# The attention and conv gates as Strassen products of tile pairs, a phase ahead of the attention, with the mixing gates alone filling the attention

## The chip, the cores and the metric

The kernel runs on one core of one Trainium2 chip. The metric is the device time of one execution in microseconds; lower is better. The times are medians of several runs. One execution was also recorded by the hardware profiler, and all views below are of that one.

## The reference, cut to what matters

One layer of a streaming encoder is applied to 1024 new frames and 32 frames of running streams, 1056 tokens in all (`TT`), with model width 1024. Ten groups of columns of one input projection are formed from the normed input `h`; the change concerns two of them, `ga` and `gb`:

```python
q, k, v, logf = ...                     # attention inputs; q and k are RMS-normed per head
ga = cols(OFF_GA, ATTN_WIDTH)           # gate of the attention branch
u  = cols(OFF_UA) * sigmoid(cols(OFF_UB))   # input of the causal depthwise convolution, 31 taps
gb = cols(OFF_GB, CONV_WIDTH)           # gate of the conv branch
ma, mb = cols(OFF_MA), cols(OFF_MB)     # gates that mix the two branches
...
ya = (o_attn * silu(ga)) @ w_pa
yb = (silu(layernorm(conv)) * silu(gb)) @ w_pb
y  = x + (sigmoid(ma) * ya + sigmoid(mb) * yb) @ w_out
```

All of it is float32. There are 16 heads of 64 channels, causal over the 1024 new frames.

## The kernel before, in words

Every float32 projection is made of three passes on TensorE: a matrix is held as a rounded part and a remainder (`xh`, `xl` for the input, `wh`, `wl` for a weight tile), and hi x hi, lo x hi and hi x lo are summed. `mms` (L102) issues these three matmuls for one of eight blocks of the contraction (`kt`). `steps` makes one tile of 128 output channels: three chunks of 352 tokens, each 8 blocks x 3 matmuls = 24 matmuls in one PSUM bank, and then an evacuation. One `yield` of `steps`, three matmuls, is called a step below, and 24 steps are a tile. A weight tile (512 KB) is loaded by `load_raw`, rounded by ScalarE (`wh`, L91), and its remainder is made by GpSimd (`wl`, L94) in `split_w`.

The stages follow one another in the program: `u` tiles and `v`, then `k` and `q` tiles (`qk`, with three further `u` tiles in between), the last `u` tile, the eight `ga` tiles, the attention, two tiles that are left over, and the three output projections. On TensorE the order is the program's order throughout. Up to the attention VectorE and ScalarE are in the program's order too; in the attention a scheduler orders them, and GpSimd and the DMA queue on SyncE are ordered by it everywhere.

The depthwise convolution runs on VectorE beside the projections: 30 `scalar_tensor_tensor` instructions a channel tile (the taps, L264). `beat()` is called at each step, adds a stage's rate (`R_U`, `R_QK`, `R_G`, `R_A`) to a credit and issues taps while the credit lasts. `later(n, fn)` runs `fn` n steps on.

The attention goes through `seq`: 16 heads x 8 blocks of 128 queries, and four `Sample`s for the running streams, 132 in all. A block has three parts: `scores` (matmuls into one of two `psS` buffers, the row maximum on VectorE L943, the exponential on ScalarE L946, the reciprocal L948, the scaling of `P` on GpSimd L949), `turn` (transposes of `P` on TensorE L966, copies of them by ScalarE L970 and VectorE L971), and `values` for two blocks at once (L982, L983; evacuated at L987, L988, gated at L993). In each round the program issues the scores of three blocks ahead, the turn of this block, four steps of gate projections from the generator `filler` (`fill(4)`), and the values of two blocks back. The filler holds 22 tiles (`NFILL`): the eight `gb` tiles and 14 of the 16 `ma` and `mb` tiles. It has one PSUM bank, `pq`; a chunk is evacuated by a copy (L771), and the next chunk writes the same bank:

```python
start(seq[0]); fill(8); start(seq[1]); fill(4); start(seq[2])
for n, b in enumerate(seq):
    start(seq[n + 3]); b.turn(); fill(4); seq[n - 2].values()      # cut
```

Eight steps are a chunk, so with fills of eight and four every chunk ends at the end of a fill. Head 0's operands are loaded while the `ga` tiles run.

## Time and profile before

| | |
|---|---|
| median of 3 runs | 1394.41 us (1393.71 to 1394.59) |
| span of the profiled execution, first to last instruction | 1392.1 us; its time as a run lies about 2.3 us above, by the median |
| TensorE busy | 1384.3 us, 99% of the span |
| VectorE, ScalarE, GpSimd busy | 906.5, 642.7, 623.2 us |
| granted TensorE clock | 1.000 |
| `ga` stage | about 510 to 598.6 us |
| attention | 598.6 to 1086.8 us |

A row of the timeline or of a group names the line, the engine, the operation, output and inputs by the program's names, shape and count. Matmuls are pipelined: a row's duration runs into the next row's, so the pace of a stream of matmuls is read from the distance of the starts, not from the durations.

### The profile page before, as it was taken

To read this page: it belongs to the slowest core of one execution; us is meant where nothing else is said; L and a number is where in the kernel's file an instruction comes from. 1 tells how busy PE (TensorE), PEld (TensorE's weight loads), DVE (VectorE), ACT (ScalarE), POOL (GpSimd) and SP (SyncE) were. 2 spreads that over 40 slices of the span, in tenths; PEclk is the share of its full clock that TensorE was granted. 3 is DMA by queue.
4 is the path that set the end of the run, shared out by engine and by line. 5 is a ranking of instruction groups with operands and counts; after the bars stand their busy time and mean duration, and the time that the engine had idled before them with its cause. 6 is when DMAs were issued, how large, how long until landed. Compare 5 with 4: busy or idle time off the path is not lost.

```text
span 1392.1 us, 24733 instructions
## 1 busy us (share of the span) xinstructions
PE 1384.3 (99%) x9382; PEld 1346.1 (97%) x9382; DVE 906.5 (65%) x1280; ACT 642.7 (46%) x1318; POOL 623.2 (45%) x669
## 2 busy tenths in 40 slices
PE   8999999999999999999999999999999999999999
PEld 7999999999999999999999999999999999999998
DVE  6687787888898999657766767655555487132111
ACT  6333434646464642245555556655555556222100
POOL 2324254657575875443333444343433257254320
PEclk9999999999999999999999999999999999999999
DMA  5253442424342374344545556454642779444431
GB/s 182 93 179 116 153 136 97 155 85 144 98 164 88 124 207 141 116 124 123 144 137 169 155 147 175 118 152 124 174 134 86 266 265 289 135 150 141 143 107 47
DMA packets 110615, 201.24 MB, mean 145 GB/s; under 512 B 17377, under 2 KB 74593, under 8 KB 110497
## 3 DMA queue, kind: packets, MB, share of 16 engines
q1 hardware_dynamic: 110352, 199.60, 45.7%
q8 instruction: 74, 1.21, 0.4%
q14 instruction: 45, 0.36, 0.1%
q10 hardware_dynamic: 144, 0.07, 0.0%
HBM read 129.78 MB, written 69.84 MB: 143 GB/s over the span
## 4 chain that ended last, share of the span: by engine, by line
PE 97%; DVE 1%; ACT 1%; DMA 0%; issue 0%; POOL 0%; SPq 0%; DVEq 0%; POOLq 0%; ACTq 0%
PE pj L102 71%; PE pjv L592 7%; PE ptr L966 5%; PE po L982 3%; PE po L983 3%; PE psS L938 3%; PE psS L939 2%; PE psS L941 1%; PE pst L716 1%; PE pst L715 1%; PE ptx L434 0%; DMA xtok<-xt 0%; ACT xh L436 0%; PE pjs L549 0%; DVE xl L437 0%
## 5 line engine op out<-in xcount | busy, mean ns | idle before, releaser
L102 PE MATMUL pj<-xh,wh 128*128 128x352 f32 (+2 forms) x1536 | 509.3, 332 | 0.4 <-ACT t L771 0.3
L102 PE MATMUL pj<-xl,wh 128*128 128x352 f32 (+2 forms) x1536 | 494.9, 322 | 0.2 <-DVE xl L437 0.2
L102 PE MATMUL pj<-xh,wl 128*128 128x352 f32 (+2 forms) x1536 | 493.2, 321 | 0.0
L94 POOL TENSOR_TENSOR wl<-raw,wh 128x384 fp32r<-128x384 f32 (+1 forms) x258 | 318.6, 1262 | 234.9 <-ACT wh L91 209.6
L264 DVE SCALAR_TENSOR_TENSOR y<-u,vec_t,y 128x1086 f32<-128x1086 f32 x240 | 378.3, 1577 | 11.5 <-ACT y L261 8.2
L102 PEld LDWEIGHTS pj<-xh,wh 128*128 128x128 f32 x1536 | 289.0, 188 | 3.4 <-issue 0.8
L102 PEld LDWEIGHTS pj<-xl,wh 128*128 128x128 f32 x1536 | 288.7, 188 | 1.4 <-DVE xl L437 1.2
L102 PEld LDWEIGHTS pj<-xh,wl 128*128 128x128 f32 x1536 | 289.4, 188 | 0.2 <-DVE wl L456 0.2
L949 POOL TENSOR_SCALAR P<-P,nm 128x128 f32<-128x128 f32 (+7 forms) x128 | 99.0, 773 | 230.6 <-DVE nm L948 203.1
L943 DVE TENSOR_REDUCE nm<-psS 128x1 f32<-128x128 f32 (+7 forms) x128 | 96.4, 754 | 71.9 <-PE psS L941 70.5
L91 ACT CAST wh<-raw 128x1024 fp32r<-128x1024 f32 x86 | 90.1, 1048 | 112.2 <-PE pj L102 81.0
L970 ACT CAST pth<-ptr 128x512 fp32r<-128x512 f32 (+1 forms) x192 | 89.1, 481 | 81.2 <-PE ptr L966 80.9
L971 DVE TENSOR_TENSOR ptl<-ptr,pth 128x512 fp32r<-128x512 f32 (+1 forms) x192 | 103.3, 550 | 24.0 <-ACT pth L970 22.3
L946 ACT ACTIVATE P<-psS,nm 128x128 f32<-128x128 f32 (+7 forms) x128 | 95.3, 744 | 35.0 <-DVE nm L943 30.3
L733 POOL TENSOR_TENSOR ql<-qn,qh 128x352 fp32r<-128x352 f32 (+1 forms) x48 | 64.6, 1346 | 69.2 <-ACT qh L732 49.8
L966 PE MATMUL ptr<-ident,P 128*128 128x128 f32 x576 | 85.0, 275 | 0.0
L982 PE MATMUL po<-pth,V 128*128 128x256 f32 x320 | 79.0, 283 | 0.0
L983 PE MATMUL po<-ptl,V 128*128 128x256 f32 x320 | 78.6, 281 | 0.0
L592 PE MATMUL pjv<-vwh,xh 128*128 128x260 f32 x256 | 72.5, 283 | 0.0
L592 PE MATMUL pjv<-vwl,xh 128*128 128x260 f32 x256 | 72.5, 283 | 0.0
L592 PE MATMUL pjv<-vwh,xl 128*128 128x260 f32 x256 | 72.3, 283 | 0.0
L938 PE MATMUL psS<-KB,QB 128*128 128x256 f32 (+2 forms) x192 | 67.9, 355 | 0.0
(213 smaller groups left out, 2460.8 us busy)
## 6 DMA issues: line engine op xcount, KB each, us to landing
raw<-wf SPq DMA_DIRECT2D x88, 512.0 KB
s_v<-vb SPq DMA_DIRECT2D x32, 256.0 KB
QB<-s_q SPq DMA_DIRECT2D x32, 256.0 KB
KB<-s_k SPq DMA_DIRECT2D x32, 256.0 KB
V<-s_v SPq DMA_DIRECT2D x16, 512.0 KB
kT<-qn SPq DMA_DIRECT2D x8, 528.0 KB
s_ga<-t SPq DMA_DIRECT2D x24, 176.0 KB
s_gb<-t SPq DMA_DIRECT2D x24, 176.0 KB
```

The lines of the kernel that those rows point to most:

```text
L94: nc.gpsimd.tensor_sub(wl[:, k0:k1, :], raw[:, k0:k1, :], f32(wh[:, k0:k1, :]))
L102: nc.tensor.matmul(ps, a[:, kt, :], b(kt, sl), start=(first and n == 0), stop=(last and n == N - 1))
L264: t = nc.vector.scalar_tensor_tensor(y, u[:, i:i + CW], w, y, op0=ALU.mult, op1=ALU.add)
L592: nc.tensor.matmul(ps[:, :VC], a, b, start=(n == 0), stop=(n == 23))
L938: nc.tensor.matmul(ps[:, b, :wm], QB[:, qsl], KB[:, ksl], start=True, stop=False)
L943: nc.vector.tensor_reduce(nm[:, 0:1], ps[:, :nb, :w], axis=AX.XY, op=ALU.max, negate=True)
L946: nc.scalar.activation(P[:, :nk].rearrange("p (b w) -> p b w", b=nb), ps[:, :nb, :w], AF.Exp, bias=nm[:, 0:1], accum_out=nm[:, 1:2])
L949: nc.gpsimd.tensor_scalar(P[:, :nk], P[:, :nk], nm[:, 2:3], 1.0, op0=ALU.mult, op1=ALU.mult)
L966: nc.tensor.transpose(pt[:, 128 * j:128 * j + 128], P[:, 128 * (4 * u + j):128 * (4 * u + j) + 128], ident)
L971: nc.vector.tensor_sub(ptl[:, js, qo], p3, f32(pth[:, js, qo]))
L982: nc.tensor.matmul(po[:, :256], V[:, j, :], pth[:, j, :], start=(j == 0), stop=False)
L983: nc.tensor.matmul(po[:, :256], V[:, j, :], ptl[:, j, :], start=False, stop=(j == njb - 1))
```

## The change

The 16 tiles of `ga` and `gb` are made as eight pairs of neighbouring tiles. A pair is a product of a 256 x 1024 weight matrix with the 1024 x 1056 input; cut in halves in each direction it is a 2 x 2 block product, and it is made with seven block products instead of eight (Winograd's form of Strassen's method). A block product is 4 contraction blocks x 3 passes x 2 chunks of 264 tokens, 24 matmuls; a pair is 168 matmuls of 264 columns where two tiles were 144 of 352.

The sums of quarters of the input (`xf`, and the third form, which is written over a quarter of `xh` and `xl`) are made once: `forms_of_x` in the `qk` stage on GpSimd and VectorE, `third_form` at the start of the first pair. The overwritten quarter is saved to `s_b` in DRAM and loaded back behind the last pair's fourth product. The sums of quarters of the weights (`sa`, `sb`) are made by VectorE for each pair, the rounding and remainders of seven half tiles by ScalarE and GpSimd, and the block products are combined at the evacuation, mostly by VectorE adds. All eight PSUM banks belong to the pairs in this phase.

All pairs run ahead of the attention. The filler of the attention then holds 14 tiles of `ma` and `mb`; the steps of a round are 4 or 5 (4.9 on average in the first 34 rounds, 4.5 afterwards) until the 14 tiles are used up. Head 0 is loaded behind the last pair, and the first eight filler steps stand ahead of the first scores. Several buffers move to a shared pool.

The diff, cut to its core:

```diff
-NFILL = 22
-R_U, R_V, R_QK, R_G, R_A = 0.25, 0.17, 0.19, 0.27, 0.12
+NFILL = 14
+R_U, R_V, R_QK, R_S, R_A = 0.25, 0.17, 0.19, 0.22, 0.12
+HT = TT // 2
+HC = HT // 2
+SPAIRS = [(g, 2 * i) for g in ("ga", "gb") for i in range(4)]
...
+    def forms_of_x():
+        xf.extend(ar.tile([128, 2, 4, HT], F32R, name="xf", tag=f"s{i}") for i in range(3))
+        for i, x in enumerate((xh, xl)):
+            nc.sync.dma_start(s_b[i], f32(x[:, 0:4, HT:]))
+        def part(j):
+            b11, b12, b21, b22 = [x32(nc.gpsimd, j + k, hf) for k in (0, 4) for hf in (0, 1)]
+            made = ((b11, 1), (b22, 2), (b21, 0))
+            def sums():
+                pace["credit"] -= 2.7
+                nc.vector.tensor_sub(b11, b12, b11)
+                nc.vector.tensor_sub(b22, b22, b11)
+                nc.vector.tensor_sub(b21, b21, b22)
+                for t, i in made:
+                    nc.scalar.copy(xf[i][:, 0, j, :], t)
+                later(5, lows)
...
+            later(26, sums)
...
+        if f == 5:
+            forms_of_x()
...
+    class Pair:
+        def split(self, i, src, n=2):
...
+            nc.scalar.copy(wh[:, :4 * n, :], src)
+            with tc.high_priority(offset=3000):
+                for k in range(0, 4 * n, 4):
+                    nc.gpsimd.tensor_sub(wl[:, k:k + 4, :], src[:, k:k + 4, :], f32(wh[:, k:k + 4, :]))
...
+        def product(self, i):
+            tag, wi, half, mov = PRODUCTS[i]
...
+            for c in range(2):
+                for kt in range(4):
+                    h, l = mov(kt, c)
+                    k = 4 * half + kt
+                    for n, (a, x) in enumerate(((wh, h), (wl, h), (wh, l))):
+                        nc.tensor.matmul(ps[:, c, :HC], a[:, k, :], x, ...)
+                    beat()
+                    yield
+            later(2, lambda: self.evac(i, ps[:, :, :HC]))
...
+    pps.close()
+    ps4 = pool("ps4", 1, stack=pS, space=PS)
+    pace["rate"] = R_S
+    for k, p in enumerate(pairs):
+        nxt = pairs[k + 1] if k + 1 < len(pairs) else None
+        later(2, lambda: p.made(5))
+        if k == 0:
+            pace["credit"] -= 5.0
+            later(1, lambda: third_form((0, 1)))
...
+        for i in range(7):
+            if nxt:
+                if i == 0:
+                    nxt.load()
+                for m, (ai, at) in enumerate(((3, 2), (4, 1), (5, 2), (5, 4), (6, 2))):
+                    if ai == i:
+                        later(at, lambda m=m: nxt.made(m))
+            for _ in p.product(i):
+                pass
+            if not nxt and i == 3:
+                for a, x in enumerate((xh, xl)):
+                    nc.sync.dma_start(f32(x[:, 0:4, HT:]), s_b[a])
...
-        if f == 5:
-            heads[0].load()
-        for _ in gate_steps("ga", f, pj):
-            pass
...
+    heads[0].load()
+    pq = pool("pq", 1, stack=p2, space=PS)
...
-    fills = [("gb", f) for f in range(8)] + [(g, f) for g in ("ma", "mb") for f in range(8)]
+    fills = [(g, f) for g in ("ma", "mb") for f in range(8)]
...
+    fill(8)
     start(seq[0])
-    fill(8)
+    fill(4)
     start(seq[1])
     fill(4)
     start(seq[2])
+    share = 0.0
     for n, b in enumerate(seq):
...
+        share += 4.9 if n < 34 else 4.5
+        n_fill = int(share)
+        share -= n_fill
...
             b.turn()
-            fill(4 if b.i > 2 or b.head.h != 8 else 0)
+            fill(n_fill)
```

More of the change, by code (lines that the diff above doesn't have):

```diff
@@ L488, in build @@
         plan.extend([("k", f), ("q", f)])
-    plan.extend([("ub", 7), ("ua", 7)] + [("ga", f) for f in range(8)] + [("gb", 0)])
+    plan.extend([("ub", 7), ("ua", 7)])
     V, G = nc.vector, nc.gpsimd
@@ L802, in build, with third_form, third_low @@
+    def third_form(js):
+        for j in js:
+            t, b = third[j]
+            nc.vector.tensor_sub(t, b, t)
+            nc.scalar.copy(xh[:, j, HT:], t)
+    def third_low(js):
+        for j in js:
+            nc.vector.tensor_sub(xl[:, j, HT:], third[j][0], f32(xh[:, j, HT:]))
     cvt[0] = u7p
     pace["rate"] = R_U
-    u_proj(7, pj)
-    assert not late
-    pqk.close()
-    pv.close()
-    hp = pool("hp", 2, stack=p2, side="right")
-    heads = [Head(h) for h in range(H)]
+    pS = ExitStack()
@@ L821, in build @@
     order.close()
+    pS.close()
     prw.close()
     pcv.close()
-    pps.close()
+    rawp[:] = [wp]
+    hp = pool("hp", 1, stack=p2, side="right")
+    heads = [Head(h) for h in range(H)]
+    heads[0].load()
+    pq = pool("pq", 1, stack=p2, space=PS)
     es.enter_context(tc.manual_schedule(engines={E.PE}))
```

186 lines of the change are left out of this document (153 added, 33 removed).

## The prediction

> **What bounds the kernel now.** I read the page first, then the busy times by stretch, then the chain that ended last.
>
> ```profile
> span 1392.1 us, 24733 instructions
> PE 1384.3 (99%) x9382; PEld 1346.1 (97%) x9382; DVE 906.5 (65%) x1280; ACT 642.7 (46%) x1318; POOL 623.2 (45%) x669
> PEclk9999999999999999999999999999999999999999
> PE 97%; DVE 1%; ACT 1%; DMA 0%; issue 0%; POOL 0%; SPq 0%; DVEq 0%; POOLq 0%; ACTq 0%
> ```
> ```profile
> core 0: us, PE busy (x) PEld busy (x) DVE busy (x) ACT busy (x) POOL busy (x), PEclk, DMA share, GB/s
> 510.00:600.00 90.00, 90.00 (x569) 89.96 (x568) 66.26 (x46) 23.91 (x37) 40.88 (x32) 1.00 0.48 141
> 900.00:1000.00 100.00, 100.00 (x745) 94.31 (x744) 53.98 (x121) 55.34 (x131) 36.21 (x67) 1.00 0.51 146
> ```
>
> TensorE is the chain, at the full granted clock, in the `ga` stage (510 to 600 us) and in the attention alike. So whatever shortens TensorE's stream shortens the kernel, and whatever makes TensorE wait lengthens it by as much. The attention has this cover only because filler steps stand in every round: in the second stretch VectorE and ScalarE are busy for 54 and 55 of 100 us. The change works on both sides: it takes columns from TensorE, and it takes eight tiles of filler out of the attention.
>
> **The products.** The pace comes from evacuations of a dense stream, each behind 24 matmuls: the `ga` chunks (352 columns) and those of `v` (260 columns).
>
> ```profile
> L769 ACT ACTIVATE t<-pj x12: 463/465/468, 534.0 to 575.9; 128x352 f32<-128x352 f32 x12
> L598 ACT COPY vf<-pjv x12: 372/372/375, 87.3 to 119.1; 128x256 f32<-128x256 f32 x12
> ```
>
> Eleven distances in 41.9 us are 3.81 us each, 158.7 ns a matmul; eleven in 31.8 us are 2.89 us, 120.5 ns a matmul. A column thus costs 0.415 ns, and a matmul of 264 columns 122.1 ns. Before, 16 tiles x 72 x 158.7 ns = 182.8 us; after, 8 pairs x 168 x 122.1 ns = 164.1 us: **18.7 us less**. So 7/8 of the columns is worth 10% of the time, since 192 more matmuls each pay a fixed part. If a column cost all there is (0.451 ns) it would be 22.7 us; these are the ends.
>
> **The switch of chunks inside a fill.** The filler has one PSUM bank. Before, chunks of eight steps end at the end of a fill, and scores, transposes or values stand ahead of the next chunk. The start of the attention shows a switch with little between:
>
> ```profile
> 602.61 0.33 PE L102 MATMUL pj<-xl,wh 128*128 128x352 f32 x1
> ...
> 603.01 0.45 ACT L771 COPY t<-pj 128x352 f32<-128x352 f32 x1 [1.01 <-ACT P L946]
> ...
> 603.52 0.43 PE L102 MATMUL pj<-xh,wh 128*128 128x352 f32 x1 [0.28 <-ACT t L771]
> ...
> 603.78 0.32 PE L102 MATMUL pj<-xh,wl 128*128 128x352 f32 x1
> ```
>
> From the start of a chunk's last matmul to that of the next chunk's first pass 0.91 us, with ScalarE idle beforehand; 0.16 us is the normal distance, so the switch costs 0.75 us, and 0.10 us more at the second matmul (0.26 instead of 0.16). The new fills are four or five steps, so chunk ends fall within them. In the built order of TensorE's instructions 32 of the 42 chunks of the attention begin right behind the previous chunk's last matmul. Nothing behind a waiting matmul can pass it on TensorE: the next scores, transposes and values are queued there, and VectorE, ScalarE and GpSimd wait for them. ScalarE is busy 55% of the time with operations of some 0.5 us, so I add 0.10 us for a copy that finds it busy: 32 x 0.95 = **30 us more**. Ends: 32 x 0.75 = 24 us, and 32 x 1.25 = 40 us where the copy mostly stands behind an exponential.
>
> **The half without filler.** 14 tiles are 336 steps. 16 go ahead of the first round, 34 rounds take 4.9, and the remaining 153 steps last 34 rounds at 4.5: the filler ends in round 69 of 132, which the built order shows too. The last 63 rounds have nothing but their own matmuls. What these heads cost now is read between the last evacuation of head 7 and that of head 15:
>
> ```profile
> L987 ACT COPY ot<-po x33: 363/365/371, 850.8 to 1087.0; 64x256 f32<-64x256 f32 x33
> ```
> ```profile
> L971 DVE TENSOR_TENSOR ptl<-ptr,pth 128x512 fp32r<-128x512 f32 (+2 forms) x94 | 51.0, 555 | 12.7 <-ACT pth L970 11.6 <-issue 0.4
> L949 POOL TENSOR_SCALAR P<-P,nm 128x640 f32<-128x640 f32 (+7 forms) x60 | 45.9, 765 | 116.7 <-DVE nm L948 97.3 <-PE ptr L966 7.6 <-PE pj L102 6.9
> L943 DVE TENSOR_REDUCE nm<-psS 128x1 f32<-128x768 f32 (+7 forms) x59 | 45.5, 772 | 30.7 <-PE psS L941 29.9 <-POOL ptl L957 0.3 <-POOL pth L956 0.3
> L946 ACT ACTIVATE P<-psS,nm 128x768 f32<-128x768 f32 (+7 forms) x59 | 44.7, 758 | 14.8 <-DVE nm L943 14.1
> L771 ACT COPY t<-pj 128x352 f32<-128x352 f32 x32 | 14.4, 450 | 13.3 <-PE pj L102 12.5
> L988 DVE TENSOR_TENSOR ot<-ot,po 64x256 f32<-64x256 f32 x32 | 13.3, 417 | 33.9 <-ACT ot L987 33.6
> L948 DVE RECIPROCAL nm<-nm 128x1 f32<-128x1 f32 x59 | 9.4, 160 | 17.5 <-ACT P L946 17.4
> L993 DVE TENSOR_TENSOR ot<-ot,ga 128x256 f32<-128x256 f32 x16 | 7.4, 461 | 0.4
> ```
>
> 236.2 us hold 32 chunks of 3.81 us, 122 us; TensorE's own work is 114 us. VectorE's five groups are 126.6 us. Without filler VectorE is therefore the longer engine, and even if it never paused the half would cost 127 - 114 = 13 us more. The other end comes from a gap that head 8's first blocks have in the filler now:
>
> ```profile
> 844.40 0.32 PE L102 MATMUL pj<-xl,wh 128*128 128x352 f32 x1
> ...
> 847.10 0.28 PE L966 MATMUL ptr<-ident,P 128*128 128x128 f32 x1
> ...
> 853.81 0.60 PE L966 MATMUL ptr<-ident,P 128*128 128x128 f32 x4
> ```
> ```profile
> 854.17 0.41 PE L102 MATMUL pj<-xh,wh 128*128 128x352 f32 x1
> ```
>
> From 844.56 (the end of the last step) to 854.17 are four rounds, 2.40 us a round, and they kept TensorE supplied, though it had some matmuls of the layer norm between. 62 rounds at that pace are 149 us, 35 us more than 114. Between 13 and 35 I take 143 us, **29 us more**, nearer the upper row, since VectorE in order, two score buffers and three transposed-block buffers leave some gaps. If rounds take longer than in that gap, it is a rival below. Here a rule of the Trainium skill speaks against the change: TensorE: Matmul & The Clock Gate, section "A second HAM failure mode: psum-queue depth-cycling", says that frequent short idles of TensorE between groups make its clock fall and recover. The granted clock is 1.00 in every row here, and no row has such idles for long, so that the trace does not decide it; the rival that it gives is priced below.
>
> **The seams and the loads beside the products.** Durations under load:
>
> ```profile
> L264 DVE SCALAR_TENSOR_TENSOR y<-u,vec_t,y x37: 1344/1351/3487, 509.7 to 574.8; 128x1086 f32<-128x1086 f32 x37
> L94 POOL TENSOR_TENSOR wl<-raw,wh x24: 734/1754/2068, 508.4 to 590.8; 128x384 fp32r<-128x384 f32 x16, 128x256 fp32r<-128x256 f32 x8
> L1123 DVE TENSOR_TENSOR y<-y,mean 128x1056 f32<-128x1056 f32 x8 | 14.3, 1785 | 0.0
> L971 DVE TENSOR_TENSOR ptl<-ptr,pth 128x512 fp32r<-128x512 f32 x96 | 65.6, 687 | 22.6 <-ACT pth L970 21.3 <-issue 0.4
> ```
>
> A pair lasts 20.5 us on TensorE. In it VectorE has seven or eight taps (8 x 1.35 = 10.8 us), four weight sums (like half of L1123, 4 x 0.87 = 3.5) and five adds from PSUM (like L971, 5 x 0.69 = 3.4): 17.7 us, 86%. GpSimd has seven remainders of 512 columns; at 1.75 us for 384 they are 2.34 us each, 16.4 us. Both fit, barely; half the slowest tap there (1.74 us) would make VectorE 20.8 us. I take 3 us for the phase, ends 0 and 16. The last pairs have few taps, and the weights are asked for some 8 us ahead. At the first pair GpSimd has seven remainders and two sums of the input in the 18 us from the middle of the last `u` tile to the fourth product: 16.4 + 2 x 2.4 = 21 us, so I take 3 us, ends 0 and 8. The sums of the input in the `qk` stage (16 on GpSimd, 24 operations on VectorE) are paced by the credit and take the place of taps; 1 us, ends 0 and 8. At the end of the attention the last values have no filler ahead of them: one transposed copy late, 2 us, ends 0 and 3.
>
> At the hand-over head 0's loads now stand on SyncE behind the last pair's last output, and in the built order the second half of them (the last keys) stands behind the output of the first filler chunk. A head's load now:
>
> ```profile
> 1008.76 0.45 SPq L786 DMA_DIRECT2D QB<-s_q  x1
> ...
> 1013.32 0.49 SPq L793 DMA_DIRECT2D KA<-s_ak  x1
> ```
>
> Issuing alone takes 5.0 us. The last pair's output is ready about 1 us behind its last matmul, and the first scores wait for all loads; TensorE has one chunk, 3.8 us, to run. 1 + 5 + some 3 us for the wait behind the chunk's output and the landing, less 3.8, is **5 us**, ends 2 and 10. The scores after them, the first transposes and head 1 are queued behind.
>
> **The sum.** -18.7 + 30 + 29 + 3 + 3 + 1 + 2 + 5 = +54 us. The span becomes 1392.1 + 54 = 1446 us; the runs' median lies 2.3 us above the span now, so 1394.4 + 54 = 1448 us.
>
> **The rivals.**
> 1. *The saving stands and the attention hides the rest: faster.* The switches and the half without filler would have to cost less than 18.7 - 14 = 5 us together; against it stand 0.75 us a switch and VectorE's 127 us against TensorE's 114. If ScalarE's copies and the scores ahead covered all of it, with 5 us at the seams, 1394.4 - 18.7 + 5 = 1381 us. It decides where a switch costs under 0.1 us and a round under 1.85 us. Chance 0.09, of which 0.02 is for seams of the full 14 us and a few switches, which end at no change.
> 2. *The floors alone.* Switches 24, the half 13, seams 5: +23 us, 1418 us. VectorE's pauses of 12.7 and 30.7 us in the rows above are waits for a TensorE that is itself full of filler, which speaks for it. Chance 0.20.
> 3. *The half without filler is bound by latency.* A block goes through maximum 0.77, exponential 0.76, reciprocal 0.16, scaling 0.77, then transposes and copies; with only three blocks ahead and two score buffers, waits behind other operations could make a round 2.9 us: 62 x 2.9 = 180 us, 66 instead of 29. That is +91 us, 1485 us; it decides from 2.4 us a round. Chance 0.18.
> 4. *The granted clock falls in that half*, since TensorE pauses at every block. At half the clock, TensorE's 114 us become 228; against 143 us that is 85 us more, 1533 us. The 1.00 in all rows speaks against it. Chance 0.03. The page of the Trainium skill named above gives such a fall.
> 5. *The change does not do what it says.* The built order has 1344 matmuls of 264 columns in one run, and no `gb` step in the attention, so only the promised time can be missing. No chance of its own.
>
> **How the numbers follow.** My forecast has 0.50. The range reaches from below rival 2 (1414 us) to above rival 3 (1490 us) and leaves out 1 and 4 and a part of the edges: 1414 to 1490. About 0.2% is what a measurement here can tell from no change, 2.8 us. Faster 0.07, within 0.2% 0.02 (both rival 1), slower 0.91 (all else).
>
> **What would show it.** Products at 2.9 us each between about 510 and 675 us; at the 32 switches distances of 0.9 to 1.1 us between filler matmuls, released by the copy; in the last third of the attention TensorE's own matmuls with waits for VectorE and ScalarE, VectorE busy near 90%, 2.2 to 2.4 us a round; a wait for head 0's load behind the first eight steps. I am wrong if the rounds without filler run at 1.9 us or the switches cost under 0.3 us.

## The result, and the profile after

The changed kernel takes **1501.85 us** (median of 4 runs, 1499.87 to 1504.09) where the kernel before takes 1394.5 us: ratio **1.077**, 95% interval 1.076 to 1.079. It is 107.4 us slower. The prediction said slower, by 54 us; the time lies 12 us above its range.

The page of the changed kernel, in the lines that answer to those shown of before:

```profile
span 1500.5 us, 25418 instructions
PE 1404.7 (94%) x9574; PEld 1339.9 (89%) x9574; DVE 1017.5 (68%) x1386; ACT 656.0 (44%) x1330; POOL 699.8 (47%) x699
PEclk9999999999999989999899999999999999999999
PE 45%; DVE 8%; issue 2%; ACT 2%; DMA 2%; POOL 0%; DVEq 0%; ACTq 0%; SPq 0%
```

TensorE is idle for 96 of 1500 us where it was idle for 8: it waits. The chain that ended last tells less here: its shares add up to 59%, since it leads back no further than 610 us; of what it covers TensorE is about three quarters, and VectorE comes next. The same two stretches as before, by windows (busy time of each engine with its instructions, granted clock, DMA share, GB/s):

```profile
core 0: us, PE busy (x) PEld busy (x) DVE busy (x) ACT busy (x) POOL busy (x), PEclk, DMA share, GB/s
510.00:600.00 90.00, 82.02 (x612) 81.21 (x611) 86.15 (x75) 32.48 (x47) 61.68 (x34) 0.94 0.24 86
900.00:1000.00 100.00, 92.28 (x621) 84.36 (x619) 56.76 (x110) 47.99 (x114) 33.81 (x61) 0.98 0.46 129
```

The first stretch now holds the first pairs, with VectorE busy 86 of 90 us; the second is in the filled half of the attention, and TensorE idles there too. What it waits for there is one row of the waits between 740 and 1038 us (total, times, longest):

```profile
PE pj L109 <- ACT t L816: 22.4, 31, 2.7
```

These are the ends of chunks inside a fill (32 with one at the start of the attention). The half without filler, first by the evacuations of the values in the same 64 rounds as before, then by its window and its longest waits:

```profile
L1200 ACT COPY ot<-po x33: 363/366/371, 1037.7 to 1195.3; 64x256 f32<-64x256 f32 x33
```
```profile
1038.00:1196.00 158.00, 130.41 (x976) 107.18 (x975) 122.78 (x287) 103.88 (x262) 55.36 (x121) 0.95 0.50 132
```
```profile
PE ptr L1179 <- DVE ptl L1184: 12.2, 15, 1.6
PE po L1195 <- DVE ptl L1184: 4.4, 6, 1.8
PE po L1195 <- DVE nm L1161: 3.9, 3, 1.9
PE po L1195 <- DVE ot L1206: 3.5, 2, 1.8
```

The 64 rounds take 157.6 us, 2.46 us each, where TensorE's own work is 114 us: 44 us lost. All waits in this window add up to 27 us. For the rest TensorE is busy longer than 114 us: the granted clock of 0.95 is some 16 us at half speed, at most 8 us of work by this estimate; what remains is not broken down. VectorE is named in the waits, yet it is busy only 122.8 of 158 us.

The places ahead of the attention, the first row from the kernel before, the rest from the changed kernel:

```profile
400.00:500.00 100.00, 100.00 (x628) 99.97 (x627) 90.08 (x83) 57.94 (x108) 72.05 (x48) 1.00 0.37 123
```
```profile
400.00:500.00 100.00, 91.55 (x550) 87.56 (x549) 93.69 (x83) 54.01 (x103) 84.82 (x59) 1.00 0.31 107
524.00:550.00 26.00, 18.48 (x119) 17.88 (x118) 25.60 (x25) 6.57 (x9) 16.75 (x10) 0.80 0.13 42
550.00:600.00 50.00, 49.54 (x407) 49.33 (x406) 47.78 (x41) 18.43 (x25) 33.37 (x16) 1.00 0.31 109
600.00:650.00 50.00, 47.87 (x392) 47.45 (x391) 49.03 (x41) 14.57 (x20) 37.93 (x20) 1.00 0.30 106
650.00:707.00 57.00, 54.29 (x441) 53.45 (x440) 43.10 (x39) 13.57 (x16) 29.98 (x19) 1.00 0.37 128
```

The counts of matmuls tell the loss: 78 fewer in the key stage, some 12 us at 0.16 us each; at the first pair 119 x 0.121 us = 14.4 of 26 us, 11.6 lost; in the other pairs, counted in the same way, 0.8, 2.7 and 3.7 us (7 in all). VectorE is busy 94 to 98% of each of these windows but the last, where it is 76%. The start of the kernel loses some 5 us as well: the first matmul of `v` stands at 77.0 us instead of 71.6. At the hand-over to the attention:

```profile
PE psS L1151 <- DMA KB<-s_k: 9.1, 1, 9.1
PE psS L1152 <- DMA KA<-s_k: 3.8, 1, 3.8
```
```profile
714.00:729.00 15.00, 5.18 (x19) 4.76 (x19) 1.70 (x3) 0.46 (x2) 1.38 (x1) 0.54 1.00 247
```

Head 0's keys are late by 9.1 and 3.8 us, and the granted clock is 0.54 in this stretch, so that the work between and behind the waits runs slowly as well; I put the loss at some 15 us.

### The profile page after: what moved, and what is told of

Same layout as the page of the kernel before. It is cut to its first block, busy times and chain, and to the rows that moved or that the text cites. A ratio compares the mean times of both kernels' runs of the same rounds, so it can differ in the third digit from the quotient of the medians.

```text
span 1500.5 us, 25418 instructions
## 1 busy us (share of the span) xinstructions
PE 1404.7 (94%) x9574; PEld 1339.9 (89%) x9574; DVE 1017.5 (68%) x1386; ACT 656.0 (44%) x1330; POOL 699.8 (47%) x699
## 4 chain that ended last, share of the span: by engine, by line
PE 45%; DVE 8%; issue 2%; ACT 2%; DMA 2%; POOL 0%; DVEq 0%; ACTq 0%; SPq 0%
PE pj L109 30%; PE po L1195 3%; PE ptr L1179 3%; PE po L1196 2%; DVE y L272 2%; PE psS L1151 2%; PE psS L1152 2%; DVE nm L1156 2%; PE ps L903 2%; DVE ptl L1184 1%; ACT t L816 1%; DMA QB<-s_q 1%; ACT P L1159 1%; PE psS L1154 1%; DMA KA<-s_k 0%
## 5 line engine op out<-in xcount | busy, mean ns | idle before, releaser
L109 PE MATMUL pj<-xh,wh 128*128 128x352 f32 (+3 forms) x1152 | 385.2, 334 | 27.1 <-ACT t L816 23.0
L272 DVE SCALAR_TENSOR_TENSOR y<-u,vec_t,y 128x1086 f32<-128x1086 f32 x240 | 393.7, 1640 | 13.8 <-ACT y L269 11.4
L109 PE MATMUL pj<-xh,wl 128*128 128x352 f32 (+3 forms) x1152 | 372.0, 323 | 1.8 <-POOL wl L101 1.8
L109 PE MATMUL pj<-xl,wh 128*128 128x352 f32 (+3 forms) x1152 | 373.1, 324 | 0.3 <-DVE xl L445 0.2
L101 POOL TENSOR_TENSOR wl<-raw,wh 128x384 fp32r<-128x384 f32 (+1 forms) x210 | 257.1, 1251 | 201.7 <-ACT wh L98 184.6
L109 PEld LDWEIGHTS pj<-xh,wh 128*128 128x128 f32 x1152 | 217.5, 189 | 39.0 <-ACT t L816 32.2
L109 PEld LDWEIGHTS pj<-xh,wl 128*128 128x128 f32 x1152 | 218.1, 189 | 3.7 <-POOL wl L101 3.5
L109 PEld LDWEIGHTS pj<-xl,wh 128*128 128x128 f32 x1152 | 217.6, 189 | 1.8 <-DVE xl L445 1.8
L903 PE MATMUL ps<-xf,wh 128*128 128x264 f32 x384 | 75.0, 290 | 8.5 <-DVE u L318 5.9
L1179 PEld LDWEIGHTS ptr<-ident,P 128*128 128x128 f32 x576 | 64.0, 145 | 17.6 <-DVE ptl L1184 7.3
L1195 PEld LDWEIGHTS po<-pth,V 128*128 128x128 f32 x320 | 62.2, 194 | 18.0 <-PE ptr L1179 4.9
```

The costliest lines, as they stand in the source:

```text
L101: nc.gpsimd.tensor_sub(wl[:, k0:k1, :], raw[:, k0:k1, :], f32(wh[:, k0:k1, :]))
L109: nc.tensor.matmul(ps, a[:, kt, :], b(kt, sl), start=(first and n == 0), stop=(last and n == N - 1))
L272: t = nc.vector.scalar_tensor_tensor(y, u[:, i:i + CW], w, y, op0=ALU.mult, op1=ALU.add)
L903: nc.tensor.matmul(ps[:, c, :HC], a[:, k, :], x, start=(i < 4 and kt == 0 and n == 0), stop=(kt == 3 and n == 2), skip_group_check=(i >= 4))
L1179: nc.tensor.transpose(pt[:, 128 * j:128 * j + 128], P[:, 128 * (4 * u + j):128 * (4 * u + j) + 128], ident)
L1195: nc.tensor.matmul(po[:, :256], V[:, j, :], pth[:, j, :], start=(j == 0), stop=False)
```

## The experiments

Theory: three costs of comparable size add up, namely the switches inside fills (about 33 us by the excess in the trace), the half without filler (about 42) and the places where the pairs meet other work (start, key stage, first pair, other pairs, hand-over: about 51), against a product that saves 19 as forecast. Rivals: the switches are hidden; rounds without filler cost the same wherever they stand; the pairs' places cost little, as predicted. All times are medians beside the kernel before on the same chip (1394.0 to 1395.1 us). Their 95% intervals reach 2 to 7 us to either side.

### The switch and the fill

The changed kernel with four steps in every round:

```diff
-        share += 4.9 if n < 34 else 4.5
-        n_fill = int(share)
-        share -= n_fill
+        n_fill = 4
```

> The changed kernel with four filler steps in every round instead of 4.9 and 4.5, so that chunks of eight steps end at the end of a fill again; the filler lasts 80 rounds instead of 69. If the 32 switches inside fills cost 1 us each (33 us by the excess that the trace shows, 30 by the prediction) and the rounds without filler 0.67 us each (42 us over 63 rounds), the time falls by 33 + 7 = 40 us to 1462 us. If the switches are hidden by what VectorE and ScalarE have ahead, only the 7 us are left: 1495 us. If the fills were needed at 4.9 because the rounds are short of TensorE work, it is above 1502 us.

Measured: **1464.6 us**, 37.2 us less; ratio to before 1.051 (1.048 to 1.054). At the 0.68 us a round of the trace (157.6 - 114 us over 64 rounds), 11 rounds are 7.5 us, which leaves 29.7 us for 32 switches: 0.93 us each. The rival (1495 us) is out.

The opposite edit in the kernel before, so that every second fill holds a chunk's end:

```diff
     start(seq[0])
-    fill(8)
+    fill(10)
```

> The kernel before with one edit: ten filler steps instead of eight ahead of the first round. All fills of four then begin and end in the middle of a chunk's halves, so that every second fill has a chunk's end inside it, some 62 switches more; products, filler and every other order stay. At 0.95 us a switch, as the prediction has it, 1394.4 + 59 = 1453 us (47 to 78 at 0.75 and 1.25). If a switch costs nothing because TensorE's next work stands ready anyway, 1394 us. If what slows the changed attention is the uneven fill and not the switches, 1394 us as well.

Measured: **1471.0 us**, 76.9 us more; ratio 1.055 (1.052 to 1.058). Its waits, and its clock:

```profile
PE pj L102 <- ACT t L771: 59.9, 65, 1.5
```
```profile
core 0: 1469.0 us, clock 1.000
```

65 switches cost 1.18 us each, of which 0.92 us is the wait itself. One number in the program, with all work unchanged, is worth 77 us. The switch is the cause, not an uneven fill.

The filler spread over the whole attention in whole fills of four:

```diff
-R_U, R_V, R_QK, R_S, R_A = 0.25, 0.17, 0.19, 0.22, 0.12
+R_U, R_V, R_QK, R_S, R_A = 0.25, 0.17, 0.19, 0.22, 0.24
...
-        share += 4.9 if n < 34 else 4.5
-        n_fill = int(share)
-        share -= n_fill
+        share += 80 / 131
+        n_fill = 4 if share >= 1 else 0
+        share -= share >= 1
```

> The changed kernel with fills of four whole steps in 80 of the 131 rounds, evenly spread over the whole attention (three in five), and the credit a step for the convolution doubled so that it ends in time. No switch inside a fill and no half without filler. If both costs are what the trace says (33 and 42 us), 1502 - 75 = 1427 us; with the prediction's own terms (30 and 29), 1443 us. If rounds without filler cost 0.67 us each wherever they stand, the spread gains nothing over four steps in every round: 51 such rounds, 34 us left, 1461 us. If VectorE (2.2 us a round) is covered on average, TensorE's 1.84 + 0.61 x 1.9 = 3.0 us a round hides it.

Measured: **1449.3 us**, 52.6 us less than the changed kernel; ratio 1.040 (1.037 to 1.043). Against four steps in every round the spread gains 15 us; full cover would have been 52 rounds x 0.68 = 35. Spreading helps, but the eight tiles that are gone leave some 20 us that three fills in five rounds don't win back.

### The half without filler

VectorE's subtraction of the low part taken out for heads 9 to 15:

```diff
-                nc.vector.tensor_sub(ptl[:, js, qo], p3, f32(pth[:, js, qo]))
+                if self.head.h < 9:
+                    nc.vector.tensor_sub(ptl[:, js, qo], p3, f32(pth[:, js, qo]))
+                else:
+                    nc.gpsimd.memset(f32(ptl[:, js, qo]), 0.0)
```

> The changed kernel without VectorE's subtraction of the low part of the transposed block for heads 9 to 15; GpSimd clears that part instead, so the low part is left out of the values there. TensorE's stream is unchanged. VectorE loses 50 of its 125 us in the half without filler. If that half is slow because VectorE, in order, is the longer engine (its rows are named in 25 us of TensorE's waits there), most of the 42 us that it costs go: 1502 - 30 = 1472 us. If it is bound by the latency of a block (maximum, exponential, reciprocal, scaling, copy), TensorE waits for the others instead: 1492 us or more. GpSimd's clearing adds at most 20 us of its idle time.

Measured: **1487.1 us**, 14.8 us less; ratio 1.066 (1.063 to 1.069). Between the theories, nearer to latency. What is late next, in the waits of that half:

```profile
PE po L1198 <- DMA V<-s_v: 9.5, 6, 1.8
PE ptr L1179 <- POOL P L1162: 2.0, 3, 0.9
```

With VectorE relieved, the load of a head's values takes its place: there is one buffer, the load starts when the previous head's last values are done, and only filler hid it; in the changed kernel TensorE waits 1.9 us for it in that half. So relieving VectorE of 50 us gives back a third of the loss. That the rest is the latency of a chain, shared by several stations, fits the waits that are left, but no run here takes that chain apart.

### The product alone

The 16 gate tiles as plain steps in the same place, no forms, no pairs; the attention as changed. The convolution's rate in this stage is 0.25 instead of 0.22 a step (cut):

```diff
-        if f == 5:
-            forms_of_x()
...
-    for k, p in enumerate(pairs):
...
+    for g in ("ga", "gb"):
+        for f in range(8):
+            for _ in gate_steps(g, f, pj):
+                pass
```

> The changed kernel with the 16 gate tiles ahead of the attention as 384 ordinary steps of 352 columns (72 matmuls a tile), and without the forms of the input, the weight sums and the pairs; the attention and its 14 tiles of filler as in the changed kernel. By the prediction's terms the product is worth 18.7 us less 3 + 3 + 1 us, so that this kernel takes 1502 + 12 = 1514 us. By the excess that the trace of the changed kernel shows (products 19 us quicker, but 5 at the start, 12 in the key and query stage, 12 at the first pair, 7 in the other pairs: 36), the product in this place loses 17 us and this kernel takes 1485 us.

Measured: **1466.9 us**, 34.9 us *less* than with the pairs; ratio to before 1.052 (1.049 to 1.055). The pairs lose 35 us where the prediction let them gain 7. The attention's part of the change is the rest, 72.9 us, together with the moved buffers, which this kernel keeps. The plain kernel issues head 0's loads from 684 us on, 10 us ahead of the first scores and beside its last outputs, and has no wait for them: so the hand-over belongs to the pairs too, which I had not counted in the 1485 us. How fast each product runs where nothing stops it, from this kernel and from the one without taps below:

```profile
600.00:650.00 50.00, 50.00 (x317) 50.00 (x316) 0.00 (x0) 10.40 (x18) 13.40 (x15) 1.00 0.26 89
```
```profile
600.00:650.00 50.00, 50.00 (x414) 50.00 (x413) 20.43 (x25) 14.36 (x18) 23.48 (x18) 1.00 0.29 103
```

157.7 ns a matmul of 352 columns, 120.8 ns for 264: 1152 x 157.7 - 1344 x 120.8 ns = 19.3 us. This saving is real.

### Where the pairs lose it

Four edits of the spread kernel. First, the saves and sums held back at the start:

```diff
-        for i, x in enumerate((xh, xl)):
-            nc.sync.dma_start(s_b[i], f32(x[:, 0:4, HT:]))
+        after = sides["tables"].ins
+        with tc.issue_after(after):
+            for i, x in enumerate((xh, xl)):
+                nc.sync.dma_start(s_b[i], f32(x[:, 0:4, HT:]))
```

> The spread kernel (1449.3 us) with the two saves of the input's upper half and the first sums of the input told to issue behind the activation table load in the key stage, so that they can't be pulled to the first 45 us of the kernel. If they delay the weights of the first tiles there and with them ScalarE and TensorE (3.1 us of wait and the half clock behind it, 4.7 us in all), the time falls by 4 to 5 us to 1445 us. If the start lost this for another cause, 1449 us.

Measured: **1447.2 us**, 2.1 us less, inside the interval. In its trace the saves and the first sum still stand at the start, so the edit did not make what was meant:

```profile
37.35 0.65 SPq L771 DMA_DIRECT2D s_b<-xh  x1
```
```profile
39.93 1.32 POOL L759 TENSOR_TENSOR t<-xh,xl 128x528 f32<-128x528 f32 x1 [1.72 <-DVE xl L445]
```

Nor is TensorE's wait there any other than in the changed kernel:

```profile
PE pj L109 <- ACT xh L444: 3.1, 1, 3.1
```

It decides nothing. In the kernel without GpSimd's sums, below, this wait is 0.5 us with the saves still in place, which speaks for the sums; that was not tried by itself.

Second, other charges for VectorE around the forms and the first pair:

```diff
-                pace["credit"] -= 2.7
+                pace["credit"] -= 4.5
...
             def lows():
+                pace["credit"] -= 1.0
...
-        pace["rate"] = R_QK
+        pace["rate"] = 0.225 if f < 5 else R_QK
...
+    pump(len(taps) - 62)
     cvt[0] = u7p
...
-            pace["credit"] -= 5.0
+            pace["credit"] -= 10.0
```

> The spread kernel with other charges for VectorE: the sums and lows of the forms are charged 5.5 instead of 2.7 a part, the first pair 10 instead of 5, and the convolution's taps run a little quicker before (0.225 a step). The number of operations is the same; fewer taps stand around the forms and the first pair. If those two places lose 12 us each because VectorE is late there with taps in front, half or more of it goes: 1435 to 1441 us. If VectorE is full over the whole stage from 400 to 700 us (281 of 300 us busy), the wait only moves to another place: 1447 to 1452 us.

The `pump` line issues taps ahead of the last `u` tile until 62 are left. Measured: **1436.0 us**, 13.3 us less; ratio 1.030 (1.027 to 1.033). The same operations in another order: by the places of the stages in the two traces, 9 us of this are in the key stage, where taps stood in front of what TensorE waited for, 3 us are at the hand-over, and under 1 us is at the first pair. There two taps still stand in front of the last `u` chunk, and TensorE waits 4.0 us for it.

Third, one whole filler tile ahead of head 0, and 75 instead of 80 fills in the attention (cut):

```diff
+    fills = [(g, f) for g in ("ma", "mb") for f in range(8)]
+    hx = ExitStack()
+    pqx = pool("pqx", 3, stack=hx, space=PS)
+    for _ in gate_steps(*fills.pop(0), pqx):
+        pass
+    hx.close()
...
-    fill(8)
     start(seq[0])
-    fill(4)
+    fill(8)
     start(seq[1])
```

> The spread kernel with the first of its 14 filler tiles run as one whole tile of 24 steps, with three banks, between the last pair and head 0's first scores, in place of eight steps. TensorE then has 11.4 us of work of its own while head 0's keys are loaded; 9.3 us of wait and 6 us at half the clock stood there. If the half clock follows from the pause, both go: 1449 - 13 = 1436 us (it gives back some 2 us of filler later). If only the wait is covered and the clock falls anyway, 1441 us. If the load is late for a cause that moves with the filler (SyncE behind the filler's own stores), 1449 us.

Measured: **1443.4 us**, 5.8 us less; ratio 1.035 (1.032 to 1.038). Half of what was expected. The last keys still stand on SyncE behind a store of the filler, now the tile's:

```profile
715.76 0.33 SPq L817 DMA_DIRECT2D s_ma<-t  x1
...
717.16 0.45 SPq L837 DMA_DIRECT2D KA<-s_k  x1
```
```profile
720.00:730.00 10.00, 5.05 (x21) 4.82 (x22) 3.05 (x4) 1.50 (x3) 4.01 (x4) 0.66 1.00 256
```

TensorE idles half of the ten us behind that, with all DMA engines full and the clock low again.

Fourth, GpSimd's sums of the input taken away. The helper that is edited makes 24 sums, 22 on GpSimd and two on VectorE at the first pair:

```diff
-        eng.tensor_add(t, f32(xh[:, kt, sl]), f32(xl[:, kt, sl]))
+        nc.scalar.copy(t, f32(xh[:, kt, sl]))
...
-            b11, b12, b21, b22 = [x32(nc.gpsimd, j + k, hf) ...]
+            b11, b12, b21, b22 = [x32(nc.scalar, j + k, hf) ...]
```

> The spread kernel in which GpSimd no longer adds the two halves of the input for the forms (24 sums): ScalarE copies the high half instead, so the low half is left out of the forms. VectorE's operations stay as they are. If GpSimd's sums slow VectorE beside them (taps 1.35 to 2.0 us) and this makes the key stage and the first pair late, their 24 us fall to under 10: 1433 us or less. If VectorE's own 32 added operations are too many, 1446 to 1450 us. If ScalarE's copies in order make a new wait, it is slower than 1450 us.

Measured: **1430.3 us**, 19 us less; ratio 1.026 (1.021 to 1.031). In the key stage TensorE is back from 550 to 610 matmuls:

```profile
400.00:500.00 100.00, 97.92 (x610) 97.10 (x609) 87.37 (x95) 68.34 (x131) 59.14 (x49) 1.00 0.38 132
```

In the key stage VectorE has the same operations, and some take less time: the 12 low parts of the forms (`xf`, L786) first in the changed kernel, then here, and the taps here (minimum, median, maximum ns):

```profile
L786 DVE TENSOR_TENSOR xf<-t,xf x12: 693/972/1840, 409.5 to 468.6; 128x528 fp32r<-128x528 f32 x12
```
```profile
L786 DVE TENSOR_TENSOR xf<-t,xf x12: 696/698/1465, 405.5 to 456.0; 128x528 fp32r<-128x528 f32 x12
L272 DVE SCALAR_TENSOR_TENSOR y<-u,vec_t,y x24: 1333/1952/2428, 442.3 to 527.7; 128x1086 f32<-128x1086 f32 x24
```

The low parts of the squares in the same stage (`sql`, L714) go from 877 to 544 ns at the median. The taps' median does not fall: it is 1949 ns in the changed kernel. So the sums made VectorE late through the forms and the squares more than through the taps. By the places of the stages in the traces, 10 of the 19 us are in the key stage, 5 at the start and 3 at the first pair.

Two more, on the pairs and on the hand-over. The taps that stand beside the pairs left out:

```diff
+            if pace.get("drop") and i < KC - 1:
+                return 1.0
             y = sides["y", f]
```

> The spread kernel without the convolution's remaining 50 or so taps of VectorE that stand beside the pairs (left out; the sums and saves of these tiles stay). Pairs, weight sums, remainders and the forms in the key stage are unchanged. If the first pair and the other pairs wait because VectorE is full there (95 of 100 us busy with the taps), most of their 19 us go: 1449.3 - 15 = 1434 us. If GpSimd's remainders of the weights or the forms' own operations hold them up, 1446 us.

Measured: **1442.2 us**, 7.1 us less; ratio 1.034 (1.032 to 1.036). The other pairs then run without a stop (the row of 414 matmuls above), which is their whole 7 us. The first pair does not gain, so the half of this theory that concerns it falls. Its trace in the changed kernel says why; first TensorE, then VectorE:

```profile
527.66 0.28 PE L903 MATMUL ps<-xl,wh 128*128 128x264 f32 x1
533.83 0.56 PE L903 MATMUL ps<-xf,wh 128*128 128x264 f32 x1 [5.89 <-DVE u L318]
```
```profile
528.47 0.52 DVE L318 TENSOR_TENSOR u<-pj,u 128x352 f32<-128x352 f32 x1
528.90 4.29 DVE L272 SCALAR_TENSOR_TENSOR y<-u,vec_t,y 128x1086 f32<-128x1086 f32 x2
533.11 0.58 DVE L318 TENSOR_TENSOR u<-pj,u 128x320 f32<-128x320 f32 x2
```

The second product needs banks that the last `u` tile still holds. Their evacuation stands behind the weight sums and two taps of 2.1 us on VectorE, all placed before the pairs begin; the kernel without taps keeps these two. TensorE does not wait for the remainders on GpSimd, which run beside these taps. No run moves the two taps, so that this cause is read from the trace alone.

The restore of the input left out:

```diff
-                for a, x in enumerate((xh, xl)):
-                    nc.sync.dma_start(f32(x[:, 0:4, HT:]), s_b[a])
+                pass
```

> The spread kernel without the two loads (2.16 MB) that put the upper half of the input back at the end of the pairs; the filler then works on the third form there. Order and number of all else stay. The DMA engines are full (share 1.0) from 700 to 730 us. If head 0's keys are late because the restore's bytes stand in front of theirs, 8 of the 13 us of wait and half clock go: 1441 us or less. If they are late because SyncE issues them behind the last pair's output and the first filler's store, 1449 us.

Measured: **1445.0 us**, 4.2 us less; ratio 1.036 (1.034 to 1.038). The intervals of the two kernels overlap, but the traces agree: the wait for `KB` falls from 8.4 us in the spread kernel to 5.2 us. So the restore's bytes are about a third of the hand-over. The rest is order and landing, in the changed kernel on SyncE and on TensorE:

```profile
710.22 0.52 SPq L834 DMA_DIRECT2D KB<-s_k  x1
...
715.19 0.33 SPq L817 DMA_DIRECT2D s_ma<-t  x1
...
716.67 0.45 SPq L837 DMA_DIRECT2D KA<-s_k  x1
```
```profile
720.06 0.55 PE L1151 MATMUL psS<-KB,QB 128*128 128x256 f32 x1 [9.11 <-DMA KB<-s_k]
724.37 0.55 PE L1152 MATMUL psS<-KA,QA 68*128 68x256 f32 x1 [3.77 <-DMA KA<-s_k]
```

`KB` is waited for 10 us behind its issue, and `KA` is issued behind the filler's store and waited for 8 us behind that.

### Combinations

All mends together, with two whole tiles ahead of head 0, 16 filler tiles, a convolution rate of 0.15, and pieces of two steps that never hold a chunk's end (fine). The coarse kernel has fills of four, 81 in 131 rounds (cut):

```diff
-NFILL = 14
+NFILL = 16
...
+    for _ in range(2):
+        for _ in gate_steps(*fills.pop(0), pqx):
+            pass
...
+        share += 324 / 131
+        n_fill = min(2 * int(share / 2), 8 - placed % 8)
+        share -= n_fill
+        placed += n_fill
```

> A combination: start and charges as in the two runs before (2 and 13 us), two whole filler tiles of three banks ahead of head 0 (the wait at the hand-over, 13 us in the kernel with one tile still some 7), 16 filler tiles in all, so that 14 remain for the attention, the convolution's rate there 0.15 instead of 0.24, and the filler in pieces of two steps that never hold a chunk's end, spread over all rounds. From 1449.3: -2 -13 -13, and of the 16 us that the attention still loses half: 1413 us. If the waits of the attention come from taps and not from the pieces, the coarse sister run is the same. If the two tiles missing behind the attention cover loads there, some 5 us more.

> The same combination with filler pieces of four steps in seven of ten rounds instead of pieces of two steps. If what the attention still loses are the rounds without any filler, 5 us slower than the fine one (1418 us); if VectorE's taps, the same time (1413 us).

Measured: **1437.4 us** (fine; ratio 1.030, 1.027 to 1.034) and **1443.9 us** (coarse; 1.035, 1.032 to 1.038). Both well above the sum; by the medians the finer pieces are worth some 6 us, as expected. A new wait has come behind the attention:

```profile
PE pj L109 <- ACT ah L1343: 12.9, 1, 12.9
```

The two gate tiles that the change leaves behind the attention are gone here; they covered the loads of its output.

The third form made early, on the fine combination:

```diff
+                nc.vector.tensor_sub(b12, b22, b12)
+                nc.sync.dma_start(s_c[j], b12)
...
-            third[j] = x32(eng, j, 1), x32(nc.gpsimd, j + 4, 1)
+            third[j] = [t528()]
+            nc.sync.dma_start(third[j][0], s_c[j])
```

> The fine combination with the third form of the input made in the key stage with the others, saved and loaded again, instead of eight sums (six on GpSimd) and four differences at the first pair. If the first pair is late because GpSimd and VectorE hold each other up there, its rest of some 6 us goes, and the key stage takes 1 us more: 1408 us. If the weights' own remainders are what it waits for, 1413 us.

Measured: **1440.5 us** (1.033, 1.029 to 1.036): no gain that the intervals tell. By the traces the first pair is 1.6 us shorter and the key stage 4 us longer.

One tile left behind the attention, on the fine combination:

```diff
-NFILL = 16
+NFILL = 15
```

> The fine combination (1437.4 us) with 15 filler tiles instead of 16, so that one gate tile is left behind the attention, where the trace of the combination shows TensorE waiting 12.9 us for the attention's output, with half clock behind it. One tile lasts 11.4 us: the wait falls to 2 us and the clock stays: 1437 - 14 = 1423 us, and the attention gets one tile less to fill it with: 1425 us. If the wait moves with the tile (the loads start later), 1437 us.

Measured: **1437.5 us** (1.031, 1.029 to 1.032): the wait for the output falls to 2.5 us, but the time does not fall with it. Other waits have come in the same place, behind the attention:

```profile
PE pj L109 <- POOL wl L101: 3.1, 1, 3.1
PE pj L109 <- DVE al L1344: 2.9, 5, 0.7
PE pj L109 <- ACT ah L1343: 2.5, 3, 1.2
PE pj L109 <- ACT wh L98: 2.4, 1, 2.4
```

From the last matmul of the values to the last of the kernel the traces have 301.7 us with two tiles left (the changed kernel), 306.0 us with one and 295.3 us with none. A tile is 11.4 us of work, so that some 16 us are lost there with one tile as with none. That is more than the 10 us by which the combination stands above the sum of its parts.

One tile ahead and 14 in all, which leaves two tiles behind the attention; and the plain kernel with the fill of the spread one:

```diff
-NFILL = 16
+NFILL = 14
...
-    for _ in range(2):
+    for _ in range(1):
```
```diff
     # the plain kernel
-        share += 4.9 if n < 34 else 4.5
+        share += 80 / 131
+        n_fill = 4 if share >= 1 else 0
+        share -= share >= 1
```

> The fine combination (1437.5 us) with one whole filler tile instead of two ahead of head 0 and 14 filler tiles in all, so that two gate tiles stand behind the attention as in the changed kernel. If the two tiles there are needed to cover the loads of the attention's output (12.9 us of wait with none left), the time falls to the sum of the single edits: 1449.3 - 2 - 13 - 6 - 4 = 1424 us. If one tile ahead leaves 5 us of wait for head 0's keys and the attention misses the rest, 1430 us. If the fine pieces themselves cost what they gain, 1436 us as the kernel with other charges alone. All are above the kernel before (1394.4 us).

> The kernel with the 16 gate tiles ahead as ordinary steps (1466.9 us), its 14 filler tiles in whole pieces of four steps spread over the attention as in the spread kernel. If the costs of the attention and of the pairs add, the spread gives the same 52.6 us here: 1414 us, 20 us above the kernel before, which is what eight tiles fewer of filler still cost when they are well spread. If the spread kernel's rest in the attention (16 us) comes from VectorE's late taps after the pairs, less is left: 1405 us.

Measured: **1431.2 us** (1.027, 1.025 to 1.029) and **1415.7 us** (1.015, 1.013 to 1.017). In the first the stretch behind the attention is back at 301.8 us, without a wait, and the median is 6 us lower. The second matters most. Spreading gives 51 us here and gave 52.6 us with the pairs, so the two halves of the change add; with the pairs as they are the difference is again 34 us. Even mended, the pairs stand 15.6 us above the plain tiles. No kernel here beats the one before.

## Why the prediction was wrong, by its own steps

The direction, the pace of the products, and the switches held. The sum of 54 us was 53 us too low, and the plain kernel divides it: the attention cost 73 us where the prediction had 30 + 29 + 2 = 61, and the pairs cost 35 us where it had -18.7 + 3 + 3 + 1 + 5 = -7.

- **Products, -18.7 us.** Right: 120.8 ns a matmul against 122.1 forecast, and 19.3 us saved.
- **Switches, 32 x 0.95 = 30 us.** Right: 29.7 us, when fills are made whole again. In the kernel before they cost 1.18 us each.
- **The half without filler, 29 us (143 us).** The mechanism was right, the size not: 157.6 us, 44 lost. The four rounds of head 8 were a good guide: 2.40 us a round against 2.46 measured. Two steps failed. The pace was multiplied by 62 rounds, while the 114 us that were taken off it, and VectorE's 127 us, belong to 64 (33 evacuations bound 32 pairs of blocks): at 2.40 us the upper end is 154 us, 40 more and not 35. And that row was taken for an upper end, with the forecast set below it, towards the 13 us that VectorE's work alone would cost; it was close to the rate itself. VectorE at near 90% was wrong as well: it is at 78%, and waits some 22 us for ScalarE's copies and exponentials and 9 us for TensorE. Rival 3 had the right idea and 2.9 us a round where it is 2.46.
- **The seams and the loads beside the products, 12 us in all.** This is the term that sank the prediction: by the plain kernel 54 us (34.9 and the 19.3 saved). The step that failed is that the added work was counted engine by engine, and not in the order in which VectorE does it and at the durations that it has beside GpSimd's. In the key stage it put 1 us (ends 0 and 8) on 16 sums and 24 operations that "take the place of taps"; 12 us were lost. Another order alone gave 9 us of them back, and the stage without GpSimd's sums 10 us, so that the two causes overlap. At the first pair it put 3 us on GpSimd's remainders; 11.6 us were lost, to an evacuation behind taps on VectorE. The products' phase, "Both fit, barely", 3 us (ends 0 and 16), cost 7, inside its ends: GpSimd's 2.34 us for most remainders held, but the tap, put at 1.35 us, has a median of 1.77 us there. The start of the kernel was not looked at: saves and sums that have no earlier input than `xh` and `xl` are pulled there by the scheduler, which the order of the built instructions on SyncE and GpSimd would have shown.
- **Hand-over, 5 us (2 to 10).** About 15. The landing, with the wait behind the store, was put at 3 us; with all 16 DMA engines full a load was waited for 8 to 10 us behind its issue, and the clock halves in the pause.
- **Tail, 2 us.** Nothing that was read in the traces sets it apart.
- **Rival 4, the granted clock.** Given 0.03 as a whole; it came in part. The mean clock is 0.95 over the half without filler, 0.54 at the hand-over and 0.80 at the first pair. Of the rule weighed in the prediction (the Trainium skill, TensorE: Matmul & The Clock Gate, section "A second HAM failure mode: psum-queue depth-cycling"), these runs show that 65 idles of 0.9 us, one every 8.5 us or so, leave it at 1.000; in the half with denser waits of up to 1.9 us it falls and recovers, as that rule has it, and the mean is 0.95.

The range was too narrow because the ends of the seams were taken one by one; together they held 2 to 45 us, and it reached up only for rival 3. The places measured some 51 us with the start, which is beyond even this upper end.

## What to carry to other kernels

A product with fewer columns pays only if its sums go to an engine with room: here TensorE won 19 us, and the places around the products gave back 54, some 31 of them beside VectorE and GpSimd, already at 90% and 72% in the key stage, and some 15 at the loads of the next stage. Work that looks like filler also hides loads, evacuations and latencies; before taking it away, list what is late next in every round, and keep each fill so that a single accumulation bank changes hands at its end. When two engines are near full, add up the work in the order of their queues, at durations read beside the load that the change brings.

## What the runs showed of the hardware

**VectorE and GpSimd stretch each other.** The convolution's tap in the changed kernel, early, with GpSimd busy 57 of 100 us, and beside the sums and remainders (minimum, median, maximum ns):

```profile
L272 DVE SCALAR_TENSOR_TENSOR y<-u,vec_t,y x33: 1328/1351/3474, 198.8 to 299.5; 128x1086 f32<-128x1086 f32 x33
```
```profile
L272 DVE SCALAR_TENSOR_TENSOR y<-u,vec_t,y x26: 1334/1949/2448, 437.0 to 528.9; 128x1086 f32<-128x1086 f32 x26
```

And GpSimd's remainder of a half tile in the pairs, in the changed kernel and in the one without taps there:

```profile
L866 POOL TENSOR_TENSOR wl<-raw,wh x19: 1289/2334/2432, 564.1 to 696.3; 128x512 fp32r<-128x512 f32 x19
```
```profile
L868 POOL TENSOR_TENSOR wl<-raw,wh x19: 1279/1290/2274, 558.5 to 686.1; 128x512 fp32r<-128x512 f32 x19
```

The tap's median goes from 1.35 to 1.95 us; early taps that no operation of GpSimd overlaps all take 1.33 to 1.35 us. The remainder's goes from 2.33 to 1.29 us when the taps beside it are gone, one edit with all else kept. The Trainium skill, SBUF — State Buffer, section "SBUF: two separate sides", says that an operation of VectorE with two inputs in SBUF and one of GpSimd that reads SBUF lock each other out for the whole instruction; the rows agree. So each is worth its stretched time on both engines.

**The clock follows single pauses, in steps.** At the first pair TensorE pauses for 5.9 us and the clock is 0.80 of 26 us, 10 us at half, in two stretches (530.9 to 537.7 and 544.6 to 547.9 us, both at 0.50); at the hand-over, pauses of 9.1 and 3.8 us go with 0.54 of 15 us, 14 us at half. The Trainium skill, TensorE: Matmul & The Clock Gate, section "What's actually happening", gives a window of 3413 ns for such a fall; three and four of them are an estimate of 10.2 and 13.7 us from that page, and the rows agree. A pause thus costs more than its length: behind the one at the hand-over the filler's matmuls start 0.29 us apart instead of 0.16.

**The time of the kernel with one tile ahead and 14 in all spreads.** Its four runs lie between 1425.9 and 1433.8 us, where those of the kernel before lie within 1.2 us; the runs do not show why.
